# A second layer's mixer whose weights stay in float32: single-pass matmuls in place of a three-part product

## The chip, the cores and the metric

The kernel runs on one core of one Trainium2 chip. The metric is the device time of one execution in microseconds (us); the figure for a kernel is the median of several runs. A core has a matmul engine (PE; its weight loads are shown apart as PEld), a vector engine (DVE), a scalar engine (ACT), a GpSimd engine (POOL) and DMA queues that SP issues to.

## The reference, cut to what matters

All arithmetic is float32. The program is one transformer block (attention, a recurrent branch, stick-breaking and memory attention, a gated FFN), followed by a second block of two layers. Each layer of the second block has a mixer and an FFN; tokens are 256, the width is 1024. What the change touches is layer l = 1 (the last): `_context_memory` and `_latent_mixer`.

```python
def _mem_parts(pm, p):
    k, v, kg, vg, glr = _split(pm, MEM_SPLITS)             # 256, 256, 512, 1024, 32 columns
    k = _rmsnorm(_heads_2(k, N_KV_HEADS), p['k_norm'])
    gf, gb = _gla_log_gates(glr, p['gla_w_a2'], p['gla_b_a'])
    ...
def _merge(o_att, o_gla, r, glu, gates, p):
    y_att = o_att @ p['w_att_o']
    y_gla = (_rmsnorm(o_gla, p['gla_norm']) * jax.nn.silu(r)) @ p['w_gla_o']
    y_conv = _conv_module(glu, p)                          # 31-tap depthwise conv, LN, silu, @ w_conv_o
    g_att, g_gla, g_conv = jnp.split(jax.nn.sigmoid(gates), N_BRANCH_2, axis=-1)
    return (g_att * y_att + g_gla * y_gla + g_conv * y_conv) @ p['w_out']
def _latent_mixer(h, mem, cos, sin, p):
    proj = h @ p['w_in']
    k, v, kg, vg, gf, gb = _mem_parts(proj[..., :MEM_COLS], p)
    q, qg, r, glu, gates = _rest_parts(proj[..., MEM_COLS:], p)
    k_ctx, v_ctx, s_f, s_b = mem                           # _context_memory(hc, p): same w_in, first columns
    ...                                                    # attention over 512 keys, two-way gated linear attention
# per layer l
    if last:
        mem = _context_memory(hc, p)
    x = _post(x, _latent_mixer(_modulate(x, sh1, sc1), mem, cos, sin, p), g1, ln1_g[l], ln1_b[l])
    x = _post(x, _ffn(_modulate(x, sh2, sc2), p), g2, ln2_g[l], ln2_b[l])
```

## The kernel before

Activations lie feature-major: a tile is 128 features by 256 tokens, and 8 such tiles make the width. A weight matrix is packed into **units** of 128x1024, each eight 128x128 blocks. `unit` (L434 to L441) issues one DMA of 512 KB per unit on SP's queue into `raw` (5 buffers), four units ahead of the one in use, and `load` (L443) prepares it two units ahead: ACT copies it to `whi` in a rounded type of 4 bytes that the matmul engine multiplies in one pass (`F32R` in the code), and DVE or POOL subtracts to `wlo`, the rest. `lo_eng` deals the subtractions out; in the stage of layer 1's mixer (phase `m1t`) three in five go to POOL and two to DVE. Inputs are split alike, into `hh` and `hl` (normalised tokens) or `yh` and `yl` (branch outputs).

Every projection is then a sum of three products, whi by hh, whi by hl and wlo by hh: `mm3` (features out) and `tok` (tokens out, where the input is the stationary side). One unit is 3 x 8 = 24 matmuls of 128x128 by 256 columns. Layer 1's context memory takes 17 units and its mixer 109, 126 in all or 3024 matmuls. The attention (`lg`, `pt`, `av`), the gated linear attention (`gz`, `gt`, `gs`, `ga`, `ov`) and the column sums (`st`) of the same stage multiply plain float32 tiles, and do so in both kernels.

`mix` writes the stage as generators that are stepped in turns: attention heads, the GLU projections and the 31-tap convolution (`conv`: on DVE, one scalar_tensor_tensor `ca` per tap, 248 operations), then two gated-linear-attention pairs (`gla_pair`) woven with the branch projections (`gated_all`, the gate units and the output units of a branch), and at the end the output projection. A scheduler with a cost model of its own orders the instructions on each engine before the program is built: `high_priority(offset=75)` draws a unit's split forward, and `offset=-1000` makes the taps fillers. On the chip each engine works through its list in that fixed order.

Four lines hold every row of a helper: `act` is L355, `tt` (tensor_tensor) L358, `stt` (scalar_tensor_tensor) L361 and `mm` L368; the weight DMA is L436.

## Time and profile before

| what | value |
|---|---|
| median of 3 runs | 3134.47 us (3131.35 to 3136.74) |
| the profiled execution's own time | 3138.93 us |
| its span, first to last instruction | 3137.1 us |
| mean granted clock of PE over the span | 0.949 |
| PE busy | 88% of the span |
| DVE, ACT, POOL busy | 75%, 47%, 34% |

The span is 1.8 us shorter than the execution's time, and that execution is 4.5 us longer than the median. A busy share is a mean over stages with different limits. The stage that the change touches runs from the first matmul of layer 1's context memory at 2294.1 us to the last of its output projection at 2889.6 us; the rows further down are taken from there, in four stretches: the context memory and the keys and values (to 2412.4), the attention with the first linear-attention pair (to 2590.5), the second pair (to 2697.5) and the remaining projections (to 2889.6). A granted clock of 1.0 is 2.4 GHz, of 0.5 is 1.2 GHz.

### The profile page before, as it was taken

Reading aid. Unit: us, or ns where it says so; the run is one execution under the profiler, and the core shown is the slowest. Engines: PE = TensorE matmul, PEld = TensorE weight load, DVE = VectorE, ACT = ScalarE, POOL = GpSimd, SP = SyncE. Lnnn points to the kernel's source line nnn. Section 1 sums busy time; section 2 is a strip of 40 time slices with the busy share of each in tenths; the row PEclk is TensorE's granted clock in tenths of the full one; section 3 lists DMA queues with packets and bytes.
Section 4 is the critical chain, followed back from the end, with each engine's and each line's share of the span. In section 5 each row is a group of like instructions: output and inputs, shape, how many; then the busy total and the mean of one; then the engine's idle time right before and its main releaser. Section 6 shows DMA issues by size and latency. Waiting matters only on the chain. (4 is left out here: it accounts for less than half of the span.)

```text
span 3137.1 us, 52191 instructions
## 1 busy us (share of the span) xinstructions
PE 2771.5 (88%) x20768; PEld 2652.9 (85%) x20768; DVE 2356.0 (75%) x3502; ACT 1470.0 (47%) x2189; POOL 1054.3 (34%) x727
## 2 busy tenths in 40 slices
PE   7998889988799887799999989999988887889898
PEld 6897778878798887788899988998987786888898
DVE  7598763689875999966898358779676799984554
ACT  5564346534345443355644544345455543344443
POOL 3243323343324335541203114444433334454000
PEclk9999999989899898899999999999999998999999
DMA  5454333455547554687567876745733222244353
GB/s 195 145 172 165 116 107 121 168 208 210 179 162 257 195 208 177 246 308 277 212 236 257 326 280 245 256 164 194 270 136 110 88 95 93 96 142 154 114 179 111
DMA packets 153428, 578.34 MB, mean 184 GB/s; under 512 B 17628, under 2 KB 17756, under 8 KB 146656
## 3 DMA queue, kind: packets, MB, share of 16 engines
q1 hardware_dynamic: 152496, 574.45, 51.4%
q8 instruction: 163, 2.67, 0.3%
q14 instruction: 81, 0.66, 0.1%
q10 hardware_dynamic: 688, 0.56, 0.1%
HBM read 516.73 MB, written 58.20 MB: 183 GB/s over the span
## 5 line engine op out<-in xcount | busy, mean ns | idle before, releaser
L358 POOL TENSOR_TENSOR wlo<-raw,whi 128x1024 fp32r<-128x1024 f32 (+1 forms) x323 | 838.9, 2601 | 1153.0 <-ACT whi L355 822.6
L355 ACT ACTIVATE whi<-raw 128x1024 fp32r<-128x1024 f32 (+1 forms) x776 | 806.6, 1046 | 892.3 <-PE mm L368 512.1
L358 DVE TENSOR_TENSOR wlo<-raw,whi 128x1024 fp32r<-128x1024 f32 (+1 forms) x344 | 456.9, 1330 | 264.5 <-ACT whi L355 241.7
L368 PE MATMUL mm<-hh,whi 128*128 128x256 f32 x3776 | 580.6, 295 | 39.1 <-DVE cv L358 21.4
L368 PE MATMUL mm<-hh,wlo 128*128 128x256 f32 x3776 | 563.2, 291 | 30.8 <-DVE wlo L358 28.6
L368 PE MATMUL mm<-hl,whi 128*128 128x256 f32 x3776 | 563.2, 292 | 0.0
L368 PEld LDWEIGHTS mm<-hh,whi 128*128 128x128 f32 x3776 | 515.6, 200 | 53.7 <-DVE cv L358 23.7
L368 PEld LDWEIGHTS mm<-hh,wlo 128*128 128x128 f32 x3776 | 509.3, 198 | 35.8 <-DVE wlo L358 30.6
L368 PEld LDWEIGHTS mm<-hl,whi 128*128 128x128 f32 x3776 | 510.7, 199 | 4.9 <-issue 4.1
L361 DVE SCALAR_TENSOR_TENSOR ca<-yp,pv,ca 128x256 f32<-128x256 f32 x720 | 410.0, 619 | 2.3
L361 DVE SCALAR_TENSOR_TENSOR adacc<-wada,sc,adacc 128x1024 f32<-128x1024 f32 x140 | 231.0, 1666 | 5.2 <-DMA wada<-in_wa 4.7
L368 PE MATMUL mm<-yh,whi 128*128 128x256 f32 x1152 | 180.4, 297 | 25.2 <-ACT yh L355 18.2
L368 PEld LDWEIGHTS mm<-yh,whi 128*128 128x128 f32 x1152 | 159.4, 201 | 32.7 <-ACT yh L355 22.9
L368 PE MATMUL mm<-yl,whi 128*128 128x256 f32 x1152 | 173.5, 293 | 9.8 <-DVE yl L358 6.3
L368 PE MATMUL mm<-yh,wlo 128*128 128x256 f32 x1152 | 172.1, 292 | 1.9 <-DVE wlo L358 1.6
L358 POOL TENSOR_TENSOR gF<-cum 128x128 f32<-128x128 f32 x192 | 98.6, 544 | 212.0 <-DVE cum L1176 102.4
L368 PEld LDWEIGHTS mm<-yl,whi 128*128 128x128 f32 x1152 | 157.6, 201 | 10.9 <-DVE yl L358 6.8
L368 PEld LDWEIGHTS mm<-yh,wlo 128*128 128x128 f32 x1152 | 155.9, 199 | 3.5 <-DVE wlo L358 2.0
L368 PE MATMUL mm<-hidl,whi 128*128 128x256 f32 x704 | 102.4, 286 | 2.7 <-DVE hidl L358 2.7
L368 PE MATMUL mm<-hidh,whi 128*128 128x256 f32 x704 | 102.9, 287 | 0.0
L368 PE MATMUL mm<-hidh,wlo 128*128 128x256 f32 x704 | 101.6, 286 | 0.0
L368 PEld LDWEIGHTS mm<-hidl,whi 128*128 128x128 f32 x704 | 93.1, 194 | 2.9 <-DVE hidl L358 2.9
(278 smaller groups left out, 3715.4 us busy)
## 6 DMA issues: line engine op xcount, KB each, us to landing
raw<-in_ws SPq DMA_DIRECT2D x744, 512.0 KB, 3.8
lo<-wlo SPq DMA_DIRECT2D x109, 512.0 KB, 3.3
wlo<-lo SPq DMA_DIRECT2D x109, 512.0 KB, 3.7
wada<-in_wa SPq DMA_DIRECT2D x48, 1024.0 KB, 4.9
raw<-in_ws SPq DMA_DIRECT2D x32, 384.0 KB, 3.1
memt<-in_tok SPq DMA_DIRECT2D x4, 256.0 KB, 4.4
xt<-in_tok SPq DMA_DIRECT2D x1, 1024.0 KB, 6.2
ct<-in_tok SPq DMA_DIRECT2D x1, 1024.0 KB, 5.7
```

The lines of the kernel that those rows point to most:

```text
L355: return self.nc.scalar.activation(out, in_, f, **k)
L358: return (eng or self.nc.vector).tensor_tensor(out=out, in0=a, in1=b, op=op)
L361: return self.nc.vector.scalar_tensor_tensor(out=out, in0=a, scalar=s, in1=b, op0=op0, op1=op1)
L368: return self.nc.tensor.matmul(out, lhsT=l, rhs=r, start=start, stop=stop, **k)
```

## The change

A switch `native` is on while layer 1's context memory and mixer are written. With it, `load` returns the `raw` buffer itself and no second part; `mm3` and `tok` issue one product of float32 weights and float32 input, 8 matmuls per unit in place of 24; and the tiles `hh`/`hl` and `yh`/`yl` become single float32 tiles `h` and `y`, so that the subtractions `hl` and `yl` are no longer written, nor the roundings of the weights and of `yh` where the producer can write `y` itself. The five `raw` buffers are then held until a unit's matmuls have read them. The first block, layer 0 and all FFNs keep the three-part product.

```diff
--- before.py
+++ after.py
@@ -326,6 +326,8 @@
         self.tc, self.nc, self.a, self.ctx = tc, tc.nc, a, ctx
         self.n_lo = 0
         self.late = None
+
+        self.native = False
         self.raws = []
         self.order, self.asked, self.ready = order, [], []
@@ -416,22 +418,26 @@
     def split(self, src, hi, lo, eng=None):
         self.act(hi, src)
+        if lo is None:
+            return
         self.tt(lo, src, hi.bitcast(F32), ALU.subtract, eng or self.lo_eng())
     def psplit(self, ps, hi, lo):
         self.act(hi, ps)
+        if lo is None:
+            return
         self.tt(lo, ps, hi.bitcast(F32), ALU.subtract)
     def unit(self, idx, n=1024):
         if self.order is None:
-            self.asked.append((idx, n))
+            self.asked.append((idx, n, self.native))
             return Null(), Null()
-        assert self.order[len(self.asked)] == (idx, n)
-        self.asked.append((idx, n))
+        assert self.order[len(self.asked)] == (idx, n, self.native)
+        self.asked.append((idx, n, self.native))
         while len(self.raws) + self.n_ready < min(len(self.asked) + self.AHEAD + 2, len(self.order)):
-            i, w = self.order[len(self.raws) + self.n_ready]
+            i, w, _ = self.order[len(self.raws) + self.n_ready]
             raw = self.wp.tile([P, 1024], F32, tag="raw", name="raw", bufs=5)
             self.nc.sync.dma_start(raw[:, :w], self.a["ws"][i, :, :w])
             self.raws.append((raw, w))
@@ -440,19 +446,21 @@
             self.n_ready += 1
         return self.ready.pop(0)
-    def load(self, raw, n, i, _):
+    def load(self, raw, n, i, _, native):
+        if native:
+            return raw, None
         hi = self.wp.tile([P, 1024], F32R, tag="whi", name="whi", bufs=3)
         lo = self.wp.tile([P, 1024], F32R, tag="wlo", name="wlo", bufs=3)
         kept = self.kept.pop(i, None)
         with self.tc.high_priority(offset=75):
             if kept is not None:
-                self.nc.sync.dma_start(lo.bitcast(F32), kept)
+                self.nc.sync.dma_start(lo.bitcast(F32)[:, :n], kept[:, :n])
                 self.act(hi[:, :n], raw[:, :n])
                 return hi, lo
             self.split(raw[:, :n], hi[:, :n], lo[:, :n])
-        if i < POS["gu0"] and self.order.count((i, n)) > 1:
+        if i < POS["gu0"] and self.order.count((i, n, False)) > 1:
             kept = self.kept[i] = self.dp.tile([P, 1024], F32, tag=f"lo{i}", name="lo")
-            self.nc.sync.dma_start(kept, lo.bitcast(F32))
+            self.nc.sync.dma_start(kept[:, :n], lo.bitcast(F32)[:, :n])
         return hi, lo
     def mm3(self, o, w, x, nk, xk, first=True, last=True):
@@ -460,6 +468,10 @@
         hi, lo = w
         xh, xl = x
         c = lambda t, k: t[:, k * P:(k + 1) * P]
+        if lo is None:
+            for k in range(nk):
+                self.mm(o, c(hi, k), xh(xk + k), start=first and k == 0, stop=last and k == nk - 1)
+            return
         for k in range(nk):
             self.mm(o, c(hi, k), xh(xk + k), start=first and k == 0, stop=False)
         for k in range(nk):
@@ -499,10 +511,12 @@
         ps = self.mmp.tile([P, 512], F32, tag="mm", name="mm")
         for t in range(2):
             n = 0
-            for x, part in ((hh, 0), (hl, 0), (hh, 1)):
+            parts = ((hh, 0),) if self.native else ((hh, 0), (hl, 0), (hh, 1))
+            for x, part in parts:
                 for k in range(KT):
                     wk = w[k // 4][part][:, (k % 4) * T:(k % 4 + 1) * T]
-                    self.mm(ps[:, t * T:(t + 1) * T], x[:, k, t * P:(t + 1) * P], wk, start=n == 0, stop=n == 23)
+                    self.mm(ps[:, t * T:(t + 1) * T], x[:, k, t * P:(t + 1) * P], wk, start=n == 0,
+                            stop=n == len(parts) * KT - 1)
                     n += 1
         return ps.rearrange("p (t c) -> p t c", t=2)
@@ -735,7 +749,9 @@
         for f in range(KT):
             self.act(mx[0][:, f], acc[:, f], scale=0.5)
-            self.stt(mx[1][:, f], acc[:, f], 0.5, mx[0][:, f].bitcast(F32), ALU.mult, ALU.subtract)
+            if not self.native:
+                self.stt(mx[1][:, f], acc[:, f], 0.5, mx[0][:, f].bitcast(F32), ALU.mult,
+                         ALU.subtract)
     def gated_all(self, name, h, y, acc, first, bias):
@@ -1282,31 +1298,36 @@
                             stop=jt == 1)
             self.act(S[:, :, hd], ps)
-    def new_h(self, pool=None):
+    def new_h(self, pool=None, native=False):
+        if native:
+            return (pool or self.hp).tile([P, KT, T], F32, tag="h", name="h", bufs=2), Nones()
         return tuple((pool or self.hp).tile([P, KT, T], F32R, tag="h" + c, name="h" + c) for c in "hl")
-    def modulated(self, x, ada, j, pool=None, fast=False):
+    def modulated(self, x, ada, j, pool=None, fast=False, native=False):
         got = []
-        run(self.modulate(x, ada, j, got, pool, fast))
+        run(self.modulate(x, ada, j, got, pool, fast, native))
         return got[0]
-    def modulate(self, x, ada, j, got, pool=None, fast=False):
+    def modulate(self, x, ada, j, got, pool=None, fast=False, native=False):
         sc, sh = ada[:, j * 8 + 8:j * 8 + 16], ada[:, j * 8:j * 8 + 8]
         xc = self.hp.tile([P, KT, T], F32, tag="D", name="xc")
         r = self.ln_core(x, xc, fast)
         yield
-        hh, hl = self.new_h(pool)
+        hh, hl = self.new_h(pool, native)
         got.append((hh, hl))
         for f in range(KT):
             t = self.t("ht")
             self.stt(t, xc[:, f], sc[:, f:f + 1], r, ALU.mult, ALU.mult)
             self.act(hh[:, f], t, AF.Identity, bias=sh[:, f:f + 1])
-            self.stt(hl[:, f], t, sh[:, f:f + 1], hh[:, f].bitcast(F32), ALU.add, ALU.subtract)
+            if not native:
+                self.stt(hl[:, f], t, sh[:, f:f + 1], hh[:, f].bitcast(F32), ALU.add, ALU.subtract)
             yield
     def new_y(self, bp):
+        if self.native:
+            return Tiles([bp.tile([P, T], F32, tag="y", name="y", bufs=11) for _ in range(KT)]), Nones()
         return tuple(Tiles([bp.tile([P, T], F32R, tag="y" + c, name="y" + c, bufs=11) for _ in range(KT)])
                      for c in "hl")
@@ -1422,8 +1443,11 @@
             self.act(s, ps, AF.Silu)
             for j in range(2):
                 sj = s[:, j * T:(j + 1) * T]
-                self.tt(sj, sj, qk[:, f // 2, j], ALU.mult, nc.gpsimd)
-                self.split(sj, yg[0][:, f + j], yg[1][:, f + j])
+                if self.native:
+                    self.tt(yg[0][:, f + j], sj, qk[:, f // 2, j], ALU.mult, nc.gpsimd)
+                else:
+                    self.tt(sj, sj, qk[:, f // 2, j], ALU.mult, nc.gpsimd)
+                    self.split(sj, yg[0][:, f + j], yg[1][:, f + j])
             step(conv, 2)
         g1 = gated(1, yg)
         step(g1, 3)
@@ -1433,8 +1457,9 @@
         for f in range(KT):
             t = self.t("ht")
             self.stt(t, ca[:, f], self.pvc(f"clg{l}", f), r, ALU.mult, ALU.mult)
-            self.act(t, t, AF.Silu, bias=self.pvc(f"clb{l}", f))
-            self.split(t, yc[0][:, f], yc[1][:, f])
+            self.act(yc[0][:, f] if self.native else t, t, AF.Silu, bias=self.pvc(f"clb{l}", f))
+            if not self.native:
+                self.split(t, yc[0][:, f], yc[1][:, f])
             if f in (0,2,4,6):
                 step(g1, 1)
         g2 = gated(2, yc)
@@ -1517,6 +1542,11 @@
     def __getitem__(self, i):
         return self.t[i[1]][(i[0],) + i[2:]]
+
+
+class Nones:
+    def __getitem__(self, i):
+        return None
 def program(tc, a, out, stage, order):
@@ -1555,7 +1585,7 @@
                     step(fill1, 1)
                 g = b.modulate(xt, ax0, 3, nxt)
                 weave((g, 9), (ffn, 1))
-                g = chain(b.post(ct, "l2g0", "l2b0"), b.modulate(ct, ac1, 0, nxt, h2))
+                g = chain(b.post(ct, "l2g0", "l2b0"), b.modulate(ct, ac1, 0, nxt, h2, native=True))
                 ffn = b.layer_ffn(0, nxt[2], xt, ax0, bp)
                 step(ffn, 2)
                 for i in range(9):
@@ -1568,9 +1598,11 @@
                 run(ffn, fill1)
             with b.pool("m1") as bp, b.phase("m1t", t1=4, t2=6, t4=4):
                 run(b.post(xt, "l2g0", "l2b0"))
-                h = b.modulated(xt, ax1, 0)
+                b.native = True
+                h = b.modulated(xt, ax1, 0, h2, native=True)
                 mem = b.ctx_memory(1, nxt[3], bp, rp)
                 b.mix(1, h, xt, ax1, mem, bp, bp)
+                b.native = False
         with b.pool("f1") as bp, b.phase("f1t", t1=10, t2=6):
             h = b.modulated(xt, ax1, 3, fast=True)
             run(b.layer_ffn(1, h, xt, ax1, bp))
```

Three places where the order of the built programs differs, as each is listed engine by engine (helper lines are two or more higher after the change: `mm` is L370, `tt` L360, `stt` L363).

PE, the projections behind the second linear-attention pair, before (`yh`/`yl` are a branch's output, `hh`/`hl` the normalised tokens):

```order
L368 MATMUL mm<-yh,whi 128x256 x6
L368 MATMUL mm<-yl,whi 128x256 x8
L368 MATMUL mm<-yh,wlo 128x256 x8
L368 MATMUL mm<-hh,whi 128x256 x8
L368 MATMUL mm<-hl,whi 128x256 x8
```

and the same place now (`raw` is the weight as loaded):

```order
L370 MATMUL mm<-h,raw 128x256 x6
L370 MATMUL mm<-y,raw 128x256 x8
L370 MATMUL mm<-h,raw 128x256 x8
L370 MATMUL mm<-y,raw 128x256 x8
L370 MATMUL mm<-h,raw 128x256 x8
```

Three runs of eight have become one, and nothing else stands between them.

DVE, before the second pair's gates (`ge`, `cum`, `gF`), with the convolution's taps `ca` and the weight splits `wlo`, before:

```order
L361 SCALAR_TENSOR_TENSOR qk<-qk,pv,nr 128x2x256 x2
L361 SCALAR_TENSOR_TENSOR ca<-yp,pv,ca 128x256 x4
L358 TENSOR_TENSOR wlo<-raw,whi 128x1024
L361 SCALAR_TENSOR_TENSOR ca<-yp,pv,ca 128x256 x12
L358 TENSOR_TENSOR wlo<-raw,whi 128x1024
L361 SCALAR_TENSOR_TENSOR ca<-yp,pv,ca 128x256 x11
L361 SCALAR_TENSOR_TENSOR ge<-gz,ge 128x512 x2
L1176 SCALAR_TENSOR_TENSOR cum<-ones,ge 128x256 x4
L358 TENSOR_TENSOR gF<-cum 128x128 x4
```

and now:

```order
L363 SCALAR_TENSOR_TENSOR qk<-qk,pv,nr 128x2x256 x2
L363 SCALAR_TENSOR_TENSOR ca<-yp,pv,ca 128x256 x44
L363 SCALAR_TENSOR_TENSOR ge<-gz,ge 128x512 x2
L1192 SCALAR_TENSOR_TENSOR cum<-ones,ge 128x256 x4
L360 TENSOR_TENSOR gF<-cum 128x128 x4
```

The splits are gone and more taps stand ahead of the gates: between the last mask copy `am` of the first pair and this `ge` there were 67 taps and 4 splits, and there are 92 taps and no split.

POOL, around the same pair, before (`gF` are the decay factors, which POOL and DVE share):

```order
L358 TENSOR_TENSOR gF<-cum 128x128 x4
L358 TENSOR_TENSOR wlo<-raw,whi 128x1024 x10
L358 TENSOR_TENSOR gF<-cum 128x128 x4
L358 TENSOR_TENSOR wlo<-raw,whi 128x1024
L358 TENSOR_TENSOR gF<-cum 128x2x64 x4
```

and now:

```order
L360 TENSOR_TENSOR gF<-cum 128x64x2 x4
L360 TENSOR_TENSOR gF<-cum 128x128 x8
L360 TENSOR_TENSOR gF<-cum 128x2x64 x4
```

POOL keeps its share of the factors and has no weight work left in the stage.

## Rows read from the trace of the kernel before

**Rows 1.** The page: its first line

```profile
span 3137.1 us, 52191 instructions
```

**Rows 2.** Four stretches: length; busy PE, PEld, DVE, ACT, POOL; PEclk; DMA share, GB/s

```profile
2294.10:2412.40 118.30, 95.69 (x678) 90.70 (x674) 93.73 (x104) 65.72 (x92) 41.81 (x19) 0.94 0.34 118
2412.40:2590.50 178.10, 153.52 (x1052) 144.76 (x1052) 149.20 (x281) 82.22 (x125) 65.60 (x56) 0.93 0.26 89
2590.50:2697.50 107.00, 82.99 (x567) 78.75 (x567) 105.21 (x182) 40.05 (x50) 41.41 (x43) 0.90 0.26 89
2697.50:2889.60 192.10, 168.41 (x1279) 166.53 (x1280) 145.58 (x172) 77.88 (x114) 102.25 (x50) 0.92 0.42 143
sum 595.50, PE 500.60 PEld 480.74 DVE 493.72 ACT 265.87 POOL 251.06; mean PE 125.15 PEld 120.19 DVE 123.43 ACT 66.47 POOL 62.77
```

**Rows 3.** PE groups in the stage: count, busy us, mean ns, idle before

```profile
L368 PE MATMUL mm<-hh,whi 128*128 128x256 f32 x592 | 95.4, 303 | 3.4 <-DVE gt L361 3.4
...
L368 PE MATMUL mm<-yh,whi 128*128 128x256 f32 x256 | 39.0, 295 | 2.2 <-ACT yh L355 2.2
...
L368 PE MATMUL mm<-whi,hh 128*128 128x256 f32 x160 | 24.8, 299 | 0.0
...
L368 PE MATMUL ov<-qb,S 128*128 128x256 f32 x32 | 8.2, 379 | 0.0
```

**Rows 4.** The timeline of PE, 2313 to 2318 us: start, length, what, count

```profile
2313.24 1.12 PE L368 MATMUL mm<-whi,hh 128*128 128x256 f32 x8
2314.20 1.12 PE L368 MATMUL mm<-whi,hl 128*128 128x256 f32 x8
```

**Rows 5.** The timeline of PE, 2591 to 2594 us, plain float32 tiles

```profile
2591.48 1.03 PE L368 MATMUL ov<-qb,S 128*128 128x256 f32 x4
2592.35 1.03 PE L368 MATMUL ov<-am,vg 128*128 128x256 f32 x4
```

**Rows 6.** What PE waited for in the stage: us, times, longest

```profile
PE ga L368 <- DVE gF L358: 25.2, 6, 11.8
PE mm L368 <- DVE wlo L358: 18.5, 5, 5.3
PE st L368 <- ACT hsq L355: 7.9, 2, 6.1
...
PE mm L368 <- DVE yl L358: 5.9, 1, 5.9
```

**Rows 7.** Groups of DVE in the stage

```profile
L361 DVE SCALAR_TENSOR_TENSOR ca<-yp,pv,ca 128x256 f32<-128x256 f32 x240 | 153.1, 690 | 0.7
L358 DVE TENSOR_TENSOR wlo<-raw,whi 128x1024 fp32r<-128x1024 f32 x50 | 68.9, 1378 | 26.1 <-ACT whi L355 20.2 <-ACT ge L355 4.5 <-ACT pr L355 1.0
```

**Rows 8.** The timeline of DVE, 2725 to 2745 us

```profile
2724.35 11.15 DVE L361 SCALAR_TENSOR_TENSOR ca<-yp,pv,ca 128x256 f32<-128x256 f32 x10
...
2738.87 4.43 DVE L361 SCALAR_TENSOR_TENSOR ca<-yp,pv,ca 128x256 f32<-128x256 f32 x11
```

**Rows 9.** The timeline of POOL, 2725 to 2745 us

```profile
2730.08 2.55 POOL L358 TENSOR_TENSOR wlo<-raw,whi 128x1024 fp32r<-128x1024 f32 x1
...
2743.79 1.98 POOL L358 TENSOR_TENSOR sr<-sr,qk 128x256 f32<-128x256 f32 x1 [8.57 <-ACT sr L355]
```

**Rows 10.** The group of weight splits on POOL in the stage

```profile
L358 POOL TENSOR_TENSOR wlo<-raw,whi 128x1024 fp32r<-128x1024 f32 x76 | 196.7, 2593 | 263.6 <-ACT whi L355 217.9 <-PE mm L368 24.9 <-DVE ptsb L638 7.1
```

**Rows 11.** The timeline of DVE ahead of the second pair, last mask copy

```profile
2589.74 0.72 DVE L1224 COPY_PREDICATED am<-gm,ga 128x512 f32<-128x512 uint8 x1
```

**Rows 12.** The timeline of DVE, 2600 to 2652 us

```profile
2631.03 8.72 DVE L361 SCALAR_TENSOR_TENSOR ca<-yp,pv,ca 128x256 f32<-128x256 f32 x11
2639.67 1.28 DVE L361 SCALAR_TENSOR_TENSOR ge<-gz,ge 128x512 f32<-128x512 f32 x2
```

**Rows 13.** The timeline of PE, 2635 to 2651 us

```profile
2648.54 2.08 PE L368 MATMUL ga<-gF 128*128 128x128 f32 x8 [11.80 <-DVE gF L358]
```

**Rows 14.** Granted clock (PEclk) in a stretch of 10 us

```profile
2643.00:2653.00 10.00, 4.46 (x21) 4.46 (x22) 9.86 (x18) 4.43 (x6) 5.87 (x9) 0.50 0.25 79
```

## The prediction

> **What bounds the kernel now.** I read first the share of busy time by engine, then the stage that the change touches cut into four stretches, then PE's groups and waits there, then DVE and POOL beside each other in time. The span is 3137.1 us [rows 1], the execution's own time 3138.9, the median 3134.5. Everything below is a difference made against that execution and then carried to the median.
>
> The stage takes 595.5 us, of which PE is busy 500.6 [rows 2]. So PE idles 94.9 us, and no other engine is nearer to full over the whole stage: DVE 493.7, ACT 265.9, POOL 251.1. Within the second pair DVE is busy 105.2 of 107.0 us while PE has 83.0: there DVE sets the pace. In the last stretch, PE is busy 168.4 of 192.1. The stage is thus bound by PE, with DVE over it in the middle, and the change makes PE slower and DVE freer. Which one wins is the question.
>
> PE's busy time holds a second loss. The granted clock is 0.94, 0.93, 0.90 and 0.92 in the four stretches [rows 2]; with two levels, 1.0 and 0.5, that is half clock for 2 x (0.06x118 + 0.07x178 + 0.10x107 + 0.08x192) = 91 us, which costs up to 46 us where PE works in it.
>
> **Term 1, the matmuls themselves: +72.6 us.** The stage has 592 + 256 + 160 = 1008 products of whi by the rounded input [rows 3], each with two fellows, 3024 in all; the change leaves 1008 in float32. Eight matmuls of the old kind start 2314.20 - 2313.24 = 0.96 us after the eight before [rows 4], so one costs 0.120 us and three 0.360. Plain float32 tiles of the same shape stand in the same trace: `ov` has 32 records in its group [rows 3] for 16 matmuls that the code issues, two records each; four records take 2592.35 - 2591.48 = 0.87 us [rows 5], so one float32 matmul costs 0.432 us (0.43 to 0.44 by these rows). Difference 0.072, times 1008: +72.6 us at full clock. The three products are thus not three times the one: the change takes away two of three instructions and PE gets 20% slower on them. A unit takes 3.46 us instead of 2.88, so the weight stream asks less of DMA per us; the DMA share here is 0.24 to 0.42 [rows 2], and holding `raw` through a unit's matmuls leaves three units, some 10 us, for a load. I cost that at nothing; if this cover failed, each late unit would cost what its load has left.
>
> On this the Trainium skill's page "FP8 and Floating Point Precision", section "TensorE Precision Notes", says that true float32 takes four passes through the array. Counting passes of today's 0.120 us, four against three would make it +121 us; the trace has two records of 0.216 us, 0.108 a pass, hence less than that. The measured rows stand, and the count by passes is a rival below.
>
> **Term 2, waits that end with a split: -24.4 us.** PE waited 18.5 us for `wlo` on DVE and 5.9 for `yl` [rows 6]. These operations no longer exist, and what is late next behind them, the weight DMA, was four units ahead.
>
> **Term 3, the other waits: -29.5 us.** What remains is 94.9 - 24.4 = 70.5 us. DVE loses 50 splits of 68.9 us [rows 7], and more: a tap `ca` takes 0.690 us in the mean [rows 7], yet eleven in a row take 4.43 us, 0.40 each, where POOL is idle, and ten take 11.15 us where POOL works [rows 8, 9]. POOL's 76 splits, 196.7 us [rows 10], go. If taps fell to 0.40 to 0.47 the 240 of them would need 57 to 70 us less than 240 x 0.690 = 166; the bounds are 0 (POOL's remaining factors stretch them as much) and 70.
>
> The largest wait, for the factors `gF` (25.2 us, one of 11.8) [rows 6], I walk through. From the last mask copy at 2589.74 [rows 11] to the gates at 2639.67 [rows 12] DVE took 49.9 us for 67 taps, four splits and the norm; `ga` followed 8.9 us later [rows 13]. Now: 25 more taps, +10; four splits of 1.21, -5; stretched taps, -13 (the eleven taps of 8.72 us [rows 12] alone give 4.3 at 0.40). That is 42, and 7.7 to `ga` without the split in between: 49.6 us. PE needs, from `ov` to that `ga`, 72 float32 products and 24 other float32 matmuls, 96 x 0.432 = 41.5 us, and starts 0 to 4 us behind the mask copy. Wait: 4 to 8 us, I take 6 instead of 11.8, and 7 for the pair's five smaller ones instead of 13.4: 25.2 becomes 13. The 7.9 us for `hsq` on ACT [rows 6] were ACT behind weight roundings, which are gone: 1 left. The other 37.4 us, thirteen smaller rows, are chains of norms, softmaxes and state updates; PE brings more work between their ends, but their own length hardly changes: I take 27 (bounds 20 and 40). Together 13 + 1 + 27 = 41, so -29.5.
>
> **Term 4, the clock: -25 us.** After the 11.8 us wait the clock stood at 0.50 for ten us [rows 14]. Of PE's waits in the stage 13 are 2.7 us or longer by the timeline, and of these five end with `wlo` or `yl` and three more by term 3. With some five left the 46 us become about 5/13 of it, 18, and I take 21 since slow stretches also fall on shorter waits. Bounds: 46 (nothing gained) and 10.
>
> **The sum.** 72.6 - 24.4 - 29.5 - 25 = -6.3 us: 3132.6 against that execution's 3138.9, and 3128 against the median 3134.5. Outside the stage nothing on the path moves: the last three units ahead of layer 1's FFN are split as before, eight subtractions in the FFN ahead drop out where PE is nearly full.
>
> **The rivals.** (a) *DVE's list is set for a slower PE.* The 92 taps now stand ahead of the second pair's gates in one piece. If the taps stay at 0.690 us, since POOL's factors and DVE's own two-tile operations meet as before, those 92 cost 27 us more than at 0.40, all on the wait for `gF`, and the taps in the attention, about 60, cost another 10 to 17 in PE's waits there. With the clock following the long wait that is +40 to the sum: about +34, 3168, slower. It decides from a tap of about 0.50 us. For it: DVE is full in that stretch today [rows 2]; against it: eleven taps at 0.40 [rows 8].
>
> (b) *The waits change owners but not length.* Only term 2 and half of the clock's gain come, since norms and softmaxes are chains that PE must sit out: 72.6 - 24.4 - 12 = +36, 3170. For it: 37 us of waits are of that kind; against it: PE now brings 20% more work between the same ends.
>
> (c) *Everything opens up.* PE has no wait over 3 us left: waits 25, clock 8, so 72.6 - 70 - 38 = -35, 3099. For it: POOL empties almost wholly; against: the first stretch waits on one chain from the residual to the normalised tokens.
>
> (d) *Four passes at today's pace*, +121 instead of +72.6: +42, 3177. The rows of `ov` [rows 5] speak against it, the same shape at 0.432; only a stream of hundreds of such matmuls, which this trace doesn't have, could differ.
>
> (e) *The change does not do what it says*, the float32 tiles being multiplied as the rounded ones are: 1008 x 0.120 would take 242 us out of PE and leave a chain of DVE and ACT work, some 3000 us. The tiles carry the same type as those of `ov`, so I give it 2%.
>
> **How the numbers follow.** A measurement of this kernel can tell about 0.2%, 6 us. The forecast, -20 to +8 around -6, gets 0.49: 0.27 faster by over 0.2%, 0.21 within, 0.01 slower. (a) gets 0.17 and (b) 0.12, both slower; (c) 0.14, faster; (d) 0.06, slower; (e) 0.02, faster. Faster 0.43, same 0.21, slower 0.36. The forecast's own range is 3114 to 3142. The wanted range reaches into (a), (b) and (c): 3092 to 3177 takes in their middles and leaves out the outer parts of (a) to (d), and (e), some two in ten.
>
> **What would show it.** In the profile after: a group of about 2016 records of `mm` with `raw`, 0.216 us apart (term 1); no wait for `wlo` or `yl` between layer 1's context memory and its output projection (term 2); the mean of `ca` under 0.50 us, and the longest wait for `gF` near 6 us (term 3; a wait of 20 us or more is rival (a)); a granted clock of 0.96 or more over the stage (term 4). The last stretch should take 187 to 194 us, with 423 products at 0.432 = 183 us in it, and PE nearly without a wait. Wrong would be a record apart by more than 0.22 us at full clock, weight loads that come late on five held buffers, or waits above 55 us in the stage.

## The result, and the profile after

The changed kernel takes 3093.45 us (median; 3090.85 to 3102.26) against 3133.71 us: a ratio of 0.9876, with a 95% interval of 0.9856 to 0.9897. (The kernel before had 3134.47 us in three runs when the prediction was made; here a fourth is added.) It is 40 us faster; the forecast was 6 us, and the rival that came nearest is (c), "everything opens up", at 3099.

The stage, cut at the same matmuls as in [rows 2] (length; busy PE, PEld, DVE, ACT, POOL; PEclk; DMA share, GB/s), after the change:

```profile
2291.80:2400.30 108.50, 102.59 (x472) 86.15 (x468) 56.30 (x87) 42.58 (x68) 3.28 (x4) 1.00 0.34 115
2400.30:2567.60 167.30, 161.43 (x811) 137.98 (x811) 128.29 (x326) 51.05 (x91) 18.88 (x36) 1.00 0.29 101
2567.60:2660.20 92.60, 86.55 (x418) 75.03 (x416) 76.31 (x170) 24.30 (x34) 14.91 (x32) 0.96 0.28 97
2660.20:2847.90 187.70, 187.56 (x869) 164.82 (x869) 39.98 (x74) 23.64 (x48) 10.34 (x10) 1.00 0.44 153
sum 556.10, PE 538.13 PEld 463.99 DVE 300.87 ACT 141.57 POOL 47.41; mean PE 134.53 PEld 116.00 DVE 75.22 ACT 35.39 POOL 11.85
```

556.1 us instead of 595.5: of the 43.1 us between the two profiled executions (40.3 between the medians) 39.4 are gained here. PE is busy 538.1 us, 37.5 more than before, and idles 18.0 us instead of 94.9. The clock is 1.00 in three stretches and 0.96 in one. DVE fell from 493.7 to 300.9 us and POOL from 251.1 to 47.4. In the last stretch PE is busy 187.56 of 187.70 us: there is nothing left to open.

What PE still waits for (us, times, longest), the answer to [rows 6]:

```profile
PE ga L370 <- DVE gF L360: 7.2, 4, 4.7
PE gt L1290 <- DVE gw L360: 3.2, 3, 2.1
PE st L370 <- DVE fsum L566: 2.4, 2, 1.7
PE pt L650 <- DVE nm L360: 2.0, 2, 1.3
```

The rows for `wlo`, `yl`, `hsq` and `pr` have vanished, and the longest wait is 4.7 us. The matmuls that answer to [rows 3] (count, busy, mean ns):

```profile
L370 PE MATMUL mm<-h,raw 128*128 128x256 f32 x1184 | 267.1, 379 | 0.0
L370 PE MATMUL mm<-y,raw 128*128 128x256 f32 x512 | 116.5, 384 | 0.0
L370 PE MATMUL mm<-raw,h 128*128 128x256 f32 x320 | 72.5, 379 | 0.0
```

2016 records for 1008 matmuls, none waited for. Their pace stands in PE's timeline:

```profile
2681.05 34.70 PE L370 MATMUL mm<-h,raw 128*128 128x256 f32 x160
2715.58 1.67 PE L370 MATMUL mm<-y,raw 128*128 128x256 f32 x7
```

160 records from 2681.05 to the next at 2715.58 are 0.216 us each, in a stream of hundreds as in the 16 of the trace before. On DVE, the groups that answer to [rows 7], with three that the prediction didn't look at:

```profile
L363 DVE SCALAR_TENSOR_TENSOR ca<-yp,pv,ca 128x256 f32<-128x256 f32 x240 | 102.1, 498 | 0.6
L360 DVE TENSOR_TENSOR gF<-cum 128x128 f32<-128x128 f32 x64 | 19.7, 361 | 1.7 <-PE ga L370 1.7
...
L1192 DVE TENSOR_TENSOR_SCAN cum<-ones,ge 128x256 f32<-128x256 f32 x16 | 10.5, 719 | 0.0
...
L360 DVE TENSOR_TENSOR acc<-acc,gt 128x256 f32<-128x256 f32 x16 | 6.8, 424 | 0.5
```

and the last three of them before the change:

```profile
L358 DVE TENSOR_TENSOR gF<-cum 128x128 f32<-128x128 f32 x64 | 27.4, 477 | 0.4 <-PE ga L368 0.4
...
L358 DVE TENSOR_TENSOR acc<-acc,gt 128x256 f32<-128x256 f32 x16 | 16.3, 1019 | 0.4
L1176 DVE TENSOR_TENSOR_SCAN cum<-ones,ge 128x256 f32<-128x256 f32 x16 | 16.3, 1062 | 0.0
```

Not only the taps got shorter: the same 16 sums `acc` took 16.3 us and take 6.8, the scans `cum` 16.3 and 10.5.

### The profile page after: what moved, and what is told of

Read it like the earlier page. It is cut to its first block, busy times and chain, and to the rows that moved or that the text cites. A ratio compares the mean times of both kernels' runs of the same rounds, so it can differ in the third digit from the quotient of the medians.

```text
span 3094.1 us, 49653 instructions
## 1 busy us (share of the span) xinstructions
PE 2809.3 (91%) x19760; PEld 2635.7 (85%) x19760; DVE 2152.1 (70%) x3412; ACT 1344.0 (43%) x2047; POOL 851.9 (28%) x643
## 5 line engine op out<-in xcount | busy, mean ns | idle before, releaser
L357 ACT ACTIVATE whi<-raw 128x1024 fp32r<-128x1024 f32 (+1 forms) x650 | 675.7, 1045 | 747.4 <-PE mm L370 397.8
L360 POOL TENSOR_TENSOR wlo<-raw,whi 128x1024 fp32r<-128x1024 f32 (+1 forms) x248 | 647.0, 2613 | 1010.3 <-ACT whi L357 721.2
L360 DVE TENSOR_TENSOR wlo<-raw,whi 128x1024 fp32r<-128x1024 f32 (+1 forms) x293 | 382.8, 1307 | 242.3 <-ACT whi L357 231.0
L370 PE MATMUL mm<-hh,whi 128*128 128x256 f32 x3184 | 485.7, 294 | 33.1 <-DVE cv L360 19.2
L370 PE MATMUL mm<-hh,wlo 128*128 128x256 f32 x3184 | 469.3, 290 | 19.7 <-DVE wlo L360 17.6
L370 PE MATMUL mm<-hl,whi 128*128 128x256 f32 x3184 | 475.3, 292 | 0.0
L370 PEld LDWEIGHTS mm<-hh,whi 128*128 128x128 f32 x3184 | 431.2, 198 | 46.8 <-DVE cv L360 20.9
L370 PEld LDWEIGHTS mm<-hh,wlo 128*128 128x128 f32 x3184 | 426.0, 197 | 23.2 <-DVE wlo L360 18.8
L370 PEld LDWEIGHTS mm<-hl,whi 128*128 128x128 f32 x3184 | 431.7, 200 | 4.3 <-issue 3.6
L363 DVE SCALAR_TENSOR_TENSOR ca<-yp,pv,ca 128x256 f32<-128x256 f32 x720 | 357.2, 557 | 2.2
L370 PE MATMUL mm<-h,raw 128*128 128x256 f32 x1184 | 267.1, 379 | 0.0
L370 PEld LDWEIGHTS mm<-h,raw 128*128 128x128 f32 x1184 | 222.7, 190 | 29.5 <-issue 0.4
L363 DVE SCALAR_TENSOR_TENSOR adacc<-wada,sc,adacc 128x1024 f32<-128x1024 f32 x140 | 229.9, 1659 | 7.2 <-DMA wada<-in_wa 6.8
L360 POOL TENSOR_TENSOR gF<-cum 128x128 f32<-128x128 f32 x192 | 98.2, 542 | 337.2 <-DVE cum L1192 171.3
L370 PE MATMUL mm<-yh,whi 128*128 128x256 f32 x896 | 139.7, 295 | 23.1 <-ACT yh L357 16.3
L370 PEld LDWEIGHTS mm<-yh,whi 128*128 128x128 f32 x896 | 122.6, 199 | 30.1 <-ACT yh L357 20.6
L363 DVE SCALAR_TENSOR_TENSOR gt<-gt,mm 128x256 f32<-128x256 f32 x72 | 29.9, 416 | 161.7 <-ACT gt L357 161.6
L370 PE MATMUL mm<-yh,wlo 128*128 128x256 f32 x896 | 133.2, 290 | 2.8 <-DVE wlo L360 2.8
L370 PE MATMUL mm<-yl,whi 128*128 128x256 f32 x896 | 133.0, 290 | 2.6 <-DVE yl L363 2.1
L370 PEld LDWEIGHTS mm<-yh,wlo 128*128 128x128 f32 x896 | 120.0, 197 | 4.4 <-DVE wlo L360 3.2
L370 PEld LDWEIGHTS mm<-yl,whi 128*128 128x128 f32 x896 | 120.2, 197 | 3.6 <-DVE yl L363 2.7
L370 PE MATMUL mm<-y,raw 128*128 128x256 f32 x512 | 116.5, 384 | 0.0
```

The costliest lines, as they stand in the source:

```text
L357: return self.nc.scalar.activation(out, in_, f, **k)
L360: return (eng or self.nc.vector).tensor_tensor(out=out, in0=a, in1=b, op=op)
L363: return self.nc.vector.scalar_tensor_tensor(out=out, in0=a, scalar=s, in1=b, op0=op0, op1=op1)
L370: return self.nc.tensor.matmul(out, lhsT=l, rhs=r, start=start, stop=stop, **k)
```

## The experiments

Two theories were set against each other. **A**, relief: PE waits less since DVE's list is shorter and its operations are no longer stretched while POOL works. **B**, pace: the chains of operations that PE waits for are as long as ever, but float32 products give PE a fifth more work between their ends.

**One engine's subtractions put back.** The changed kernel, with the weight subtractions of this stage issued again into tiles that nobody reads. Three runs: those of POOL alone, those of DVE alone, and the whole preparation (ACT's rounding too). In the first, the lists of PE and ACT are the same as in the changed kernel, and those of DVE and POOL but for one weight split, which moved from POOL to DVE near the stage's end. In the other two the scheduler reordered PE, ACT and DVE in many places, so the first is the cleanest of the three.

```diff
         if native:
+            if self.lo_eng() is self.nc.gpsimd:
+                spare = self.wp.tile([P, 1024], F32R, tag="wlo", name="spare", bufs=3)
+                with self.tc.high_priority(offset=75):
+                    self.tt(spare, raw, raw, ALU.subtract, self.nc.gpsimd)
             return raw, None
```

(This is the first; the second has `is not` and no engine named, so that DVE does it; the third calls `self.split` on tiles of its own for every unit.)

> The changed kernel, with the 76 subtractions of 128x1024 that POOL did in this stage written again, into a tile that nobody reads; every other engine's list is the same. Theory A (DVE's relief: PE's waits shrank because DVE's list got shorter and its operations are no longer stretched while POOL works): the taps go back from 0.498 us to about 0.65 to 0.69, DVE's busy time in the stage rises by 40 to 60 us, PE's idle time in the stage from 18 to 35 to 60 us, the time from 3093 to 3115 to 3150 us. Theory B (PE's pace: the float32 products give PE a fifth more work between the ends of the same chains, so the waits are covered whatever DVE does): the taps are stretched too, but PE's idle time stays under 26 us and the time under 3102 us.

> The changed kernel, with the 50 subtractions of 128x1024 that DVE did in this stage written again into a tile that nobody reads (some 65 us more on DVE's list), none on POOL. Theory A (DVE's relief): PE's idle time in the stage 30 to 50 us instead of 18, the time 3105 to 3130 us. Theory B (PE's pace): idle time under 26 us, the time under 3102 us.

> The changed kernel, with every weight unit of this stage also rounded on ACT and subtracted on DVE or POOL as before, into tiles that nobody reads; PE multiplies float32 and waits for none of it. Theory A (DVE's relief): all that term 3 and the clock gave is lost again, PE's idle time 50 to 75 us, the clock 0.94 to 0.96 over the stage, the time 3130 to 3165 us, no gain left against the kernel before or a loss of up to 30 us. Theory B (PE's pace): idle time 20 to 30 us, the time 3095 to 3110 us.

Measured: POOL's back, 3144.9 us (0.2 to 0.5% *slower* than the kernel before: ratio 1.0035, 1.0022 to 1.0048), in A's range. DVE's back, 3094.1 us (0.9879, 0.9856 to 0.9901): nothing lost, in B's range. All back, 3172.7 us (1.012, 1.0096 to 1.0145), above A's range. So A holds in one half only: POOL's work costs, DVE's own doesn't. B alone can't be the account, since PE's idle time went from 18 to 51 us with POOL's work back, at the same float32 products. The first kernel's stage and second pair, and PE's waits:

```profile
2598.10:2706.60 108.50, 86.76 (x418) 75.75 (x417) 94.27 (x182) 24.41 (x34) 62.07 (x43) 0.91 0.25 83
...
sum 599.50, PE 548.43 PEld 471.53 DVE 360.69 ACT 141.76 POOL 219.38; mean PE 137.11 PEld 117.88 DVE 90.17 ACT 35.44 POOL 54.84
```

```profile
PE ga L370 <- DVE gF L360: 22.9, 4, 17.3
```

With POOL's work back the stage is at 599.5 us, and PE waits 17.3 us at one `gF`; none of its waits there is for a weight load. A's account of the taps was too high: their mean is 0.540 us, where 0.65 to 0.69 was expected. With DVE's work back:

```profile
sum 555.10, PE 537.64 PEld 463.50 DVE 358.34 ACT 141.35 POOL 54.49; mean PE 134.41 PEld 115.88 DVE 89.58 ACT 35.34 POOL 13.62
```

```profile
L360 DVE TENSOR_TENSOR spare<-raw 128x1024 fp32r<-128x1024 f32 x48 | 58.9, 1226 | 87.8 <-DMA raw<-in_ws 87.7
```

(the window holds 48 of the 50). DVE is busy 358.3 us instead of 300.9 and the stage stays at 555.1 us: DVE had the room. So POOL's 76 cost 51 us where DVE's 50 cost nothing, and DVE's busy time in the run with POOL's is *as high* (360.7 us) as in the run with its own. The parts don't add up, though: all back is 28 us slower than POOL's alone, so beside POOL's work DVE's subtractions or ACT's roundings do cost. Which of them was not separated.

How POOL's work gets into DVE's time is seen ahead of the second pair, on DVE and on POOL at the same time:

```profile
2597.30 16.31 DVE L363 SCALAR_TENSOR_TENSOR ca<-yp,pv,ca 128x256 f32<-128x256 f32 x41
2613.53 0.68 DVE L367 TENSOR_SCALAR nv<-st 128x512 f32<-128x512 f32 x1
2614.14 1.51 DVE L363 SCALAR_TENSOR_TENSOR ca<-yp,pv,ca 128x256 f32<-128x256 f32 x1
2615.57 2.11 DVE L367 TENSOR_SCALAR nr<-nv 128x512 int32<-128x512 int32 x1
...
2622.59 2.12 DVE L363 SCALAR_TENSOR_TENSOR ca<-yp,pv,ca 128x256 f32<-128x256 f32 x1
...
2626.89 17.50 DVE L363 SCALAR_TENSOR_TENSOR ca<-yp,pv,ca 128x256 f32<-128x256 f32 x44
2644.32 1.27 DVE L363 SCALAR_TENSOR_TENSOR ge<-gz,ge 128x512 f32<-128x512 f32 x2
```

```profile
2601.76 15.63 POOL L360 TENSOR_TENSOR spare<-raw 128x1024 fp32r<-128x1024 f32 x2 [4.53 <-DMA raw<-in_ws]
2622.53 1.89 POOL L360 TENSOR_TENSOR spare<-raw 128x1024 fp32r<-128x1024 f32 x1 [5.13 <-DMA raw<-in_ws]
2629.62 18.76 POOL L360 TENSOR_TENSOR spare<-raw 128x1024 fp32r<-128x1024 f32 x2 [5.19 <-DMA raw<-in_ws]
2648.34 2.66 POOL L360 TENSOR_TENSOR gF<-cum 128x128 f32<-128x128 f32 x4
```

DVE's 41 taps run from 2597.3 at 0.40 us each, untouched. A subtraction that POOL starts at 2601.76 doesn't get through meanwhile: two take 15.63 us, to 2617.4 (the first 13.6 of them), where one that meets no run of taps, at 2622.53, takes 1.89 us. When the taps end (`nv`, with one input, at 2613.5) POOL comes through, and now DVE waits: one tap takes 1.51 us instead of 0.47, and `nr` 2.11. The tap beside the subtraction at 2622.53 takes 2.12. Then 44 taps again, and again POOL stands, 18.76 us for two (the first 16.5), with its share of the factors `gF` behind it. One of the two engines runs and the other stands.

These two long stands of POOL are exceptions: by the single durations, no other subtraction of the stage took more than 4.2 us. Far more often it is DVE that stands, one operation for one of POOL's: 10 of the 240 taps took over 1.3 us here. In the kernel before, 22 took 2.0 to 2.7 us, about as long as a subtraction on POOL there (2.4 in the median), and no subtraction on POOL took more than 4.5. The same place in the changed kernel:

```profile
2587.50 17.55 DVE L363 SCALAR_TENSOR_TENSOR ca<-yp,pv,ca 128x256 f32<-128x256 f32 x44
2604.92 1.33 DVE L363 SCALAR_TENSOR_TENSOR ge<-gz,ge 128x512 f32<-128x512 f32 x2
2606.11 2.79 DVE L1192 TENSOR_TENSOR_SCAN cum<-ones,ge 128x256 f32<-128x256 f32 x4
```

There `ge` starts 37.3 us after the stretch's beginning, with POOL's work back 46.2 us; `ga` follows 9.3 us after `ge` there and 12.9 here. Together (8.9 and 3.6) these are the 12.5 us by which the longest wait grew.

The Trainium skill's page "SBUF — State Buffer", section "Who interferes with whom", says that DVE and GpSimd (POOL) share a pair of memory ports by an exclusive lock held for the whole instruction, and that a DVE instruction with two inputs contends with a GpSimd one that reads. The trace agrees on who stands, and mostly on how long; that one sometimes stands for a whole run of the other's instructions and not for one of them, 16.5 us for one subtraction here, is the trace's alone. How much of the 51 us is DVE's operations and how much POOL's own queue, with `gF` behind subtractions, was not separated. At the longest wait 8.9 us are DVE's list up to `ge`. In the 3.6 us behind it both have a part: DVE's `cum` and `gF` take 3.6 us longer, and POOL's `gF`, with a subtraction between them, end 1.3 us after DVE's (0.8 in the changed kernel).

**What it takes on POOL.** In place of each subtraction two fills that read nothing, or one copy that reads one tile.

```diff
-                    self.tt(spare, raw, raw, ALU.subtract, self.nc.gpsimd)
+                    for _ in range(2):
+                        self.nc.gpsimd.memset(spare.bitcast(F32), 0.0)
```

```diff
-                    self.tt(spare, raw, raw, ALU.subtract, self.nc.gpsimd)
+                    self.nc.gpsimd.tensor_copy(spare, raw)
```

> The changed kernel with POOL's list filled as in the run that put its 76 subtractions back, but with fills: two memsets of 128x1024 (0.95 us each in the trace of before) in the place of each subtraction, which read nothing. Theory P (POOL's queue: the factors gF stand behind 76 pieces of work on POOL): the loss comes back in large part, 3115 to 3145 us, with gF late on POOL. Theory C (contention: DVE's operations and POOL's two-input operations hold each other up, and that alone is the loss): taps and other DVE operations keep the lengths that they have after the change, PE's idle time in the stage stays under 24 us, the time 3088 to 3102 us.

> The same with one copy of 128x1024 from the loaded weights in the place of each subtraction: it reads one tile and not two. If contention comes from any read of POOL (theory C1), DVE's busy time in the stage rises by about 60 us as with the subtractions and the time is 3120 to 3150 us; if it takes a two-input operation on POOL (theory C2), DVE's busy time stays within 10 us of the changed kernel's 301 us and the time is 3088 to 3105 us.

Measured: fills 3123.5 us (0.9953, 0.9926 to 0.9979), but from 3090 to 3129 from run to run; copies 3114.4 us (0.9927, 0.9903 to 0.9951). The fills' time lies in P's range, but `gF` isn't late (PE's longest wait for it is 4.7 us, as after the change), so P's mechanism is not what happened; and the time is above C's range. The fills wait for nothing, so they ran one behind another to 2434 us; the taps kept their pace, 118.3 us in all against 119.5 after the change (sums of the single durations), and the loss hangs mostly on one operation, in the second stretch, where 21.0 of the stage's 24.3 us more lie:

```profile
2417.57 15.99 DVE L367 TENSOR_SCALAR pr<-pr,rs 128x512 f32<-128x512 f32 x1
```

```profile
2410.90 23.55 POOL L455 MEMSET spare<- 128x1024 f32 x26
```

DVE's tensor_scalar `pr` started at 2417.57 and ended 0.9 us, one fill, before POOL's 26 fills did, 15.99 us for what takes 0.49; PE waited 14.2 us behind it. It is the only one of this length: five tensor_scalar operations `nr` met fills too, of which four were longer by 0.2 to 0.9 us and one by 3.2. That the one run at 3090 us of ten escaped this collision would fit, but it was not traced. The same section of the Trainium skill's page "SBUF — State Buffer" tells these cases apart: operations of DVE in a two-port mode, which tensor_scalar can enter, contend with GpSimd, those with two inputs only with a GpSimd instruction that reads. Here `pr` was held up by fills and the taps weren't, so the trace agrees; that `pr` ran in such a mode no run shows. The copies, which read, held up two-input operations again:

```profile
sum 571.70, PE 539.93 PEld 464.79 DVE 322.36 ACT 141.69 POOL 161.00; mean PE 134.98 PEld 116.20 DVE 80.59 ACT 35.42 POOL 40.25
```

```profile
L454 POOL CAST spare<-raw 128x1024 fp32r<-128x1024 f32 x73 | 115.0, 1578 | 337.1 <-DMA raw<-in_ws 337.1
```

DVE 21 us more than the changed kernel, the time 21 us more. Both theories missed their ranges. The contention is there with a single read, which is C1's mechanism, but at a third of the 60 us that C1 named, with operations that are shorter (115.0 us in all against 171.2 for the same number of subtractions).

**The relief without float32.** The changed kernel with its relief for DVE and POOL, but PE's old work: weights rounded on ACT as before, and three products of the rounded parts.

```diff
         if native:
-            return raw, None
+            hi = self.wp.tile([P, 1024], F32R, tag="whi", name="whi", bufs=3)
+            with self.tc.high_priority(offset=75):
+                self.act(hi, raw)
+            return hi, None
```

(cut; and `h` and `y` in the rounded type, each product written three times). This kernel is for its time alone: it leaves out the two products with remainders and adds the first one three times, so its sums come out tripled, which is more than the "less exact" of the expectation.

> The other way round: in this stage weights are rounded on ACT as before, nothing is subtracted on DVE or POOL, and PE multiplies the rounded weights by the rounded input three times, so PE has its old 3 x 0.120 us per block and DVE and POOL the relief of the change. What it leaves out are the two products with remainders, so its numbers are less exact. Theory A (DVE's relief): PE's idle time stays at 18 to 35 us and the time falls by most of the 72.6 us: 3025 to 3050 us. Theory B (PE's pace): the waits come back, idle time 60 to 75 us and the clock under 0.95 in the stage: 3075 to 3105 us.

Measured: 3027.4 us (0.9664, 0.9639 to 0.969).

```profile
sum 488.80, PE 467.83 PEld 450.37 DVE 299.66 ACT 259.33 POOL 52.02; mean PE 116.96 PEld 112.59 DVE 74.91 ACT 64.83 POOL 13.01
```

```profile
PE ga L370 <- DVE gF L360: 6.9, 6, 2.5
PE mm L370 <- ACT whi L357: 4.4, 3, 2.6
```

PE idles 21.0 us at its old pace, 18.0 at the slower one: the slower pace covers next to nothing, and B is out. (The scheduler reordered DVE and ACT here too.) Against this kernel the change costs 66 us in time and 70.3 us of PE's busy time. The change is thus two steps: without subtractions, -107 us; float32 in place of three rounded products, +66 us.

**No subtraction on POOL, three-part products kept.** If POOL is the cause, the kernel before needs one entry of a table only.

```diff
-LO = {"b1t": (1, 2), "b1ft": (1, 3), "m0t": (3, 5), "f0t": (1, 2), "m1t": (3, 5), "f1t": (0, 1)}
+LO = {"b1t": (1, 2), "b1ft": (1, 3), "m0t": (3, 5), "f0t": (1, 2), "m1t": (0, 1), "f1t": (0, 1)}
```

> The kernel before, with one entry changed: in this stage all 126 weight subtractions are dealt to DVE, none to POOL; the three-part products stay. If the gain of the change lies in POOL's absence (theory A as the runs so far leave it), DVE takes 76 x 1.3 = 99 us more work but its other operations lose some 90 to 110 us of holding up, so its busy time stays near 494 us and PE's waits for factors and softmaxes shrink while those for wlo grow: 3085 to 3135 us. If DVE's own list is what counts (theory B2), 99 us more on a list that is full in the second pair make the stage longer: 3145 to 3200 us.

Measured: 3072.8 us (0.9799, 0.9774 to 0.9825): 60 us faster than before and 21 faster than the change, with the arithmetic of before.

```profile
L358 DVE TENSOR_TENSOR wlo<-raw,whi 128x1024 fp32r<-128x1024 f32 x126 | 154.3, 1230 | 31.8 <-ACT whi L355 30.9 <-PE mm L368 0.3 <-issue 0.3
```

```profile
2631.30:2827.00 195.70, 155.01 (x1249) 152.47 (x1250) 158.46 (x272) 77.96 (x112) 8.00 (x8) 0.90 0.39 135
sum 527.50, PE 468.68 PEld 449.71 DVE 457.93 ACT 267.94 POOL 54.68; mean PE 117.17 PEld 112.43 DVE 114.48 ACT 66.98 POOL 13.67
```

```profile
PE st L368 <- DVE fsum L552: 30.5, 3, 27.9
```

DVE makes all 126 subtractions, 85 us more of them than before, and is busy 457.9 us instead of 493.7. Three stretches now take 331.8 us (before: 403.4), and the last one 195.7: there PE waits 27.9 us for the sum over the convolution, since the taps have slid to the end of DVE's list.

**Float32 where DVE is full, three parts where it isn't.** First the changed kernel with the last 48 units back in three parts, their subtractions on DVE; then the run before this one with float32 for the 40 units of the attention's queries, the GLU and the first gated branch alone.

```diff
+        if self.native:
+            self.native = False
+            self.lo_pool = (0, 1)
+            hs = self.new_h()
+            for f in range(KT):
+                self.act(hs[0][:, f], h[0][:, f])
+                self.tt(hs[1][:, f], h[0][:, f], hs[0][:, f].bitcast(F32), ALU.subtract)
+            h = hs
         yg = newy()
```

```diff
-LO = {"b1t": (1, 2), "b1ft": (1, 3), "m0t": (3, 5), "f0t": (1, 2), "m1t": (3, 5), "f1t": (0, 1)}
+LO = {"b1t": (1, 2), "b1ft": (1, 3), "m0t": (3, 5), "f0t": (1, 2), "m1t": (0, 1), "f1t": (0, 1)}
...
+                hn = h2.tile([P, KT, T], F32R, tag="hh", name="hn").bitcast(F32)
+                for f in range(KT):
+                    b.tt(hn[:, f], h[0][:, f].bitcast(F32), h[1][:, f].bitcast(F32), ALU.add)
...
-        ya = newy()
+        ya = self.new_y(bp, hn is not None)
+        hm = hn or h
...
-        att = self.attention(l, h, ya, kt, vt, mem, bp)
+        att = self.attention(l, hm, ya, kt, vt, mem, bp)
```

> The changed kernel, with the last 48 units of the mixer (the recurrent branch's gate input, the last two branches and the output projection) back in the three-part product, all their subtractions on DVE, none on POOL. In that stretch DVE is busy 40 of 188 us and PE waits for nothing, so the float32 products only cost there: 48 x 8 x 0.072 = 27.6 us less on PE, 60 us more on DVE, which has the room. If PE is the only bound there: 3065 to 3072 us. If the subtractions' chain (load, rounding, subtraction) shows up again, or DVE's taps of the second pair run into it: 3075 to 3095 us.

> A mixture: three-part products with all subtractions on DVE in layer 1's mixer, but float32 weights in one pass for the 40 units of the attention's queries, the GLU and the first gated branch, where DVE is full. Against the run with every subtraction on DVE, PE has 320 x 0.072 = 23 us more and DVE 40 x 1.23 = 49 us less, so the taps end earlier and the 40 us of waits for the convolution's norm in the last stretch (27.9, 6.6 and 4.5 us the longest) should go, with some of the half clock: 3045 to 3060 us. If those waits stay, 3090 to 3100.

Measured: 3076.6 us (0.9813, 0.9787 to 0.9838) and 3052.9 us (0.9747, 0.9723 to 0.9772). The first lies 17 us below the change where 21 to 28 were expected for PE alone, and so in the other range, though the late chain that this range stood for isn't there: its last stretch fell by 23.2 us (187.7 to 164.5) and the other three stayed as they were. In the profiled execution 4.0 us more lie ahead of the stage and 2.5 behind it, where the programs are nearly the same and the traces of this document differ by as much. In the second the wait for the convolution is gone:

```profile
2632.80:2797.30 164.50, 161.66 (x1253) 157.82 (x1253) 109.25 (x154) 76.37 (x112) 7.38 (x8) 1.00 0.51 177
sum 513.80, PE 490.69 PEld 452.52 DVE 412.68 ACT 227.84 POOL 50.11; mean PE 122.67 PEld 113.13 DVE 103.17 ACT 56.96 POOL 12.53
```

```profile
PE ga L370 <- DVE gF L360: 8.1, 5, 4.5
PE st L370 <- DVE fsum L569: 2.7, 2, 1.8
```

195.7 us became 164.5, and no wait is over 4.5 us.

**Elsewhere in the program.** All subtractions on DVE in layer 0's mixers too; this together with the mixture; and none on POOL anywhere.

```diff
-LO = {"b1t": (1, 2), "b1ft": (1, 3), "m0t": (3, 5), "f0t": (1, 2), "m1t": (0, 1), "f1t": (0, 1)}
+LO = {"b1t": (1, 2), "b1ft": (1, 3), "m0t": (0, 1), "f0t": (1, 2), "m1t": (0, 1), "f1t": (0, 1)}
```

(the first two), and

```diff
+LO = {"b1t": (0, 1), "b1ft": (0, 1), "m0t": (0, 1), "f0t": (0, 1), "m1t": (0, 1), "f1t": (0, 1)}
```

> The kernel before, with all weight subtractions dealt to DVE in layer 0's two mixers as well as in layer 1's; three-part products throughout. If what the last runs showed holds in general (a two-input operation on POOL costs DVE about as much as the same work on DVE itself, and comes later), layer 0's context mixer, where DVE is busy 97 to 100 of 100 us and POOL 42 to 54, gains too: 15 to 50 us under the 3073 us of the run with layer 1 alone, 3020 to 3058. If DVE there is bound by its own list, since it has more work than in layer 1, it is the same or slower: 3070 to 3110.

> Both together: the mixture of float32 and three-part products in layer 1's mixer, and all subtractions of both layers' mixers on DVE. The two gains lie in different stages, so they should add: 3053 - 48 = 3005, 2998 to 3012 us. If the stages share something (weights or clock), 3015 to 3030.

> The same with no weight subtraction on POOL anywhere, in the first block and layer 0's FFN too. There POOL takes one in two or one in three, DVE is busy 54 to 95 of 100 us and PE mostly waits for other things. If POOL's two-input work costs DVE as much as it takes off it everywhere: another 5 to 40 us less, 2965 to 3000 us. If DVE's list is the longer one there: 3005 to 3030 us.

Measured: 3025.1 us (0.9654, 0.9631 to 0.9677), 3016.1 us (0.9612, 0.9596 to 0.9627) and 2898.6 us (0.9256, 0.923 to 0.9282). The first gained 48 us as hoped. The second lies in the range for stages that share something, but that isn't shown: the mixture adds 9 us here and 20 alone; by the ratios to the kernel before on the same chip it is 0.0042 and 0.0052, which the intervals don't tell apart. The third went far past its range: another 117 us. Busy time of the whole execution, the mixture with layer 0, then without POOL:

```profile
PE 2746.3 (91%) x20448; PEld 2610.7 (87%) x20448; DVE 2253.7 (75%) x3632; ACT 1432.6 (48%) x2149; POOL 676.0 (22%) x557
```

```profile
PE 2703.5 (93%) x20448; PEld 2577.0 (89%) x20448; DVE 2210.9 (76%) x3849; ACT 1437.7 (50%) x2149; POOL 168.1 (6%) x340
```

179 more subtractions on DVE (448 before, 627 now; their group went from 573.2 to 756.9 us), and DVE is busy 43 us *less*.

## Why the prediction was right or wrong

The measured 3093.45 us lie 1.5 us inside the lower end of the wide range, 3092 to 3177, and two of the four runs lie below it. The forecast's own range, 3114 to 3142, is missed by 20 us. That the wide range held, drawn as it was to take in the middles of the rivals, is luck as far as the forecast's sum goes.

**Term 1 (+72.6) was right.** 2016 records at 0.216 us; 70.3 us of PE's busy time between the runs with the old products and the new ones. Rivals (d) and (e) are out. Term 2 (-24.4) was right as well: its rows are gone and nothing came in their place.

**Term 3 (-29.5) was the step that failed.** PE's other waits fell from 70.5 to 18.0 us, so -52.5. The walk to `gF` was near (4.7 us forecast as 6, the sum 7.2 as 13). The largest error, 16 of 23 us, is the sentence that the thirteen smaller waits are chains whose "own length hardly changes", 27 us of 37.4 left; 10.8 are. Those chains run over DVE, and POOL held up whatever was in them: `acc`, `cum`, the norms, the column squares. I had counted POOL's price on the taps alone, where many equal rows made it visible; of DVE's 192.8 us some 68 are subtractions of weights, 22 those of inputs, some 50 the taps and the other 50 spread over many small groups. The bound of 0 to 70 us that I set for the taps was right for them, and too narrow for the engine. (A slip beside it: at 0.47 us the 240 taps need 53 us less than 166, not 57. The sum doesn't use it.) The signs that I named all came, `ca` at 498 ns, the longest wait for `gF` at 4.7 us, the last stretch at 187.7 us: none of them looked at the smaller waits, so none could show this error.

**Term 4 (-25) was too small for the same reason.** With term 1 at 72.6, PE's busy time would be 573.2 at the old clock; it is 538.1, so the clock gave 35.1. I took five waits over 2.7 us to be left; one is, and one stretch of half clock (0.96 in the third stretch).

So 72.6 - 24.4 - 52.5 - 35.1 = -39.4, the stage's difference. Rival (c) had nearly named this (no wait over 3 us, waits 25, clock 8; it came to one wait of 4.7, waits of 18.0, and 35.1 from the clock where (c) counted 38) and got 0.14, because I held the chain at the stage's start to be fixed. It wasn't: the first stretch takes 108.5 us after the change, and 122.4 with POOL's work back. Rival (a) had the right suspect and the wrong direction: it asked whether POOL's few factors would go on stretching the taps. They didn't, at 44 taps in 17.5 us; but put POOL's 76 subtractions back and 51 us are lost, where (a) had priced 40. Its point of decision was blurred by a reading: a row's mean counts what overlaps with the neighbour (690 ns before, 498 after), while busy time by count gives 0.64 and 0.43 us.

What the prediction did not ask is whether the work had to leave DVE and ACT at all. It put the gain down to a shorter list on DVE; the runs show DVE's own 50 subtractions to be free where POOL's are gone, and POOL's 76 to be enough to undo the whole gain.

## What to carry to other kernels

Before work is dealt to POOL "because it idles", price it on DVE: in the trace, compare the same DVE operation where POOL works and where it is idle, over all groups and not the commonest one, and try the whole share on DVE. A change that removes work on several engines should be taken apart engine by engine before its gain is put down to the step it is named after: here the named step cost 66 us, and one table entry without it was worth more than the change.

## What the runs showed of the hardware that was not expected

DVE and POOL hold each other up. Mostly it is one operation for one: in the kernel before 22 of the 240 taps took 2.0 to 2.7 us in place of 0.47, about the length of a POOL subtraction (2.4). In a few cases one stands for a whole run of the other: beside 41 and 44 back-to-back taps single POOL subtractions took 13.6 and 16.5 us, and beside back-to-back fills one DVE operation took 16.0 us. What decides between the two was not tested. In busy time of DVE, 76 subtractions on POOL cost 60 us, as much as 50 on DVE itself (57 us). And a float32 matmul of this shape costs 0.432 us against 0.120 for the rounded type, so 3.6 times one rounded product and 1.2 times three.
